# Projecting q, k and v in transposed layout, with rotary by VectorE shuffles across partitions

## The chip, the cores and the metric

The kernel runs on one core of a Trainium2 chip. The metric is the device time of one execution in microseconds (us). The engines of the core work side by side, each on its own list of instructions in order, and wait for each other by semaphores: TensorE (PE in the profile, its weight loads PEld), VectorE (DVE), ScalarE (ACT), GpSimd (POOL) and SyncE (SP, which issues most of the transfers).

## The reference

One decoder layer: 1024 tokens, model width 1024, all in float32. The part that matters here is the attention side of the token mixer, 8 query heads and 2 key/value heads of width 64, a window of 128 tokens:

```python
h = rmsnorm(x, pre_w_mix[l]) * (1.0 + sc1) + sh1
proj = h @ w_in[l]
aq, ak, av, hq, hf, hi, hg = jnp.split(proj, _SPLITS, axis=-1)
aq = partial_rope(aq.reshape(B, T, ATT_Q_HEADS, ATT_HEAD_DIM))
ak = partial_rope(ak.reshape(B, T, ATT_KV_HEADS, ATT_HEAD_DIM))
...
attn = sliding_window_sink_attention(aq, ak, av, attn_sinks[l])
attn = rmsnorm(attn, attn_out_w[l])
```

partial_rope turns only the first 16 of a head's 64 dimensions: with x1 the first eight and x2 the second eight, it gives x1·cos − x2·sin and x2·cos + x1·sin; the other 48 pass. In the window attention each block of 128 queries sees its own and the previous block of keys, with a mask and a sink per head in the softmax. Behind it follow a gated recurrence (hq, hf, hi, hg), an output projection and a squared-ReLU MLP; the change does not touch them.

## The kernel before

Tokens are cut into two halves of 512 and eight blocks of 128 (tb 0 to 7); the model width into eight column blocks of 128 (kb). Each float32 product is made of three products of split numbers, high by high, high by low, low by high, so each weight and each h has a tile "hi" and a tile "lo" (h: hhi, hlo; weights wq…h, wq…l, wkv…h, wkv…l). ScalarE writes hhi, POOL a helper f, VectorE hlo.

Stage 1, up to 57 us: x is normalised, turned and split for the first half, one kb at a time, and q and k/v of token blocks 0 to 3 are accumulated in step with it by first_mm: the h slice of one block is the weight operand, wq (512 columns) or wkv (256) moves, so the result has tokens on partitions. Stage 2, the loop with proj3, brings the second half of h and projects q of blocks 4 and 5 meanwhile. The rest of the second half's q and k/v are fillers: kv_later and q_later put single matmuls into a list feed_q, and feed(us) takes matmuls from it worth so many microseconds. Behind them the list holds values(tb), products pv for the recurrence.

Stage 3, from 72 to 185 us, is the attention. attention(tb) is a generator of eight steps per block: turn q and k by TensorE (pqT, pkT) so that the head dimension lies on partitions, and copy them out; scores sc for two head pairs; the mask (copy_predicated), maximum mx, its negative nm and sd on VectorE, eight exponentials on ScalarE, the sums den and their reciprocal, and the scaling of comb, half by VectorE, half by POOL; turn the probabilities (pT) and split them into pc (own block) and pp (previous block) on VectorE; the output oT; its squares' sum sqr, its sum over partitions ssp and ssc; the inverse root r_att by POOL, dg, rb. The loop over t interleaves the steps of blocks t, t+1 and t+2, with feed between them. VectorE also splits weights whv in it and sums products of the modulation (macc, by mod_sums).

The order is written by hand. pin holds an engine's instructions in the order of the program for a while; otherwise Queue.issue places an instruction behind a named one (marks: "kT", "sd", "rb", "dg"), and the scheduler fills in. Rotary before (rope) works on tokens on partitions: four small instructions (16 of 64 columns each head) for q and four for k of a block, on VectorE for blocks 0 and 1, on POOL for the others, with tables cosT and sinT of 64 KB each.

All instructions go through one helper, so nearly all rows of the profile carry its line, L39; rows are told apart by their tiles.

## Time and profile before

| | |
|---|---|
| time, median of 3 runs | 1082.05 us (1081.71 to 1082.11) |
| the profiled execution | 1081.48 us, span 1079.6 us |
| mean granted TensorE clock | 0.997 |
| TensorE busy | 1066.4 us, 99% of the span |
| VectorE busy | 806.3 us, 75% |
| ScalarE busy | 589.1 us, 55% |
| POOL busy | 372.8 us, 35% |
| 57 to 72 us | PE 15.00 of 15.0, DVE 13.07 |
| 72 to 105 us | PE 32.36 of 33.0, DVE 23.39 |
| 105 to 185 us | PE 79.35 of 80.0, DVE 64.21 |
| 185 to 1079 us | PE 886.06 of 894.0, DVE 668.86 |

The profile is of one execution. A row of a timeline gives the start, the busy time and the instruction with its output and inputs; in brackets follows the idle time of the engine before it and what ended that. The chain of waits goes back from the last instruction to what released each step. Spans of POOL are rough.

### The profile page before, as it was taken

To read this page: it belongs to the slowest core of one execution; us is meant where nothing else is said; L and a number is where in the kernel's file an instruction comes from. 1 tells how busy PE (TensorE), PEld (TensorE's weight loads), DVE (VectorE), ACT (ScalarE), POOL (GpSimd) and SP (SyncE) were. 2 spreads that over 40 slices of the span, in tenths; PEclk is the share of its full clock that TensorE was granted. 3 is DMA by queue.
4 is the path that set the end of the run, shared out by engine and by line. 5 is a ranking of instruction groups with operands and counts; after the bars stand their busy time and mean duration, and the time that the engine had idled before them with its cause. 6 is when DMAs were issued, how large, how long until landed. Compare 5 with 4: busy or idle time off the path is not lost.

```text
span 1079.6 us, 16058 instructions
## 1 busy us (share of the span) xinstructions
PE 1066.4 (99%) x5449; PEld 873.6 (81%) x5449; DVE 806.3 (75%) x1329; ACT 589.1 (55%) x1215; POOL 372.8 (35%) x497
## 2 busy tenths in 40 slices
PE   8999999999999999999999999999999999999996
PEld 6887777888888888888888888888888888888885
DVE  4877787879756655468867767786678887899776
ACT  4556544456547654566655555555664544456434
POOL 1263211233325643423444444443333333300014
PEclk9999999999999999999999999999999999999998
DMA  9904012444112342424676777767898888998537
GB/s 358 347 21 142 16 30 88 141 145 148 48 60 82 99 161 85 139 79 134 223 263 220 267 232 247 255 224 247 310 373 291 280 295 269 305 313 272 171 98 140
DMA packets 102979, 205.74 MB, mean 191 GB/s; under 512 B 13168, under 2 KB 13936, under 8 KB 102896
## 3 DMA queue, kind: packets, MB, share of 16 engines
q1 hardware_dynamic: 87408, 157.14, 43.1%
q0 software_dynamic: 15200, 47.20, 14.5%
q8 instruction: 43, 0.70, 0.3%
q10 hardware_dynamic: 288, 0.36, 0.1%
q14 instruction: 40, 0.33, 0.1%
HBM read 149.60 MB, written 55.05 MB: 190 GB/s over the span
## 4 chain that ended last, share of the span: by engine, by line
PE 93%; DMA 3%; DVE 2%; ACT 1%; issue 0%; SPq 0%; DVEq 0%; POOL 0%; ACTq 0%; POOLq 0%
PE pda L39 16%; PE pua L39 14%; PE pdc L39 8%; PE po L39 8%; PE puc L39 7%; PE phf L39 4%; PE phg L39 4%; PE pu L39 4%; PE phq L39 4%; PE pdb L39 4%; PE pv L39 4%; PE pub L39 4%; PE pq L39 2%; DMA wa<-wada 2%; PE pk L39 1%; PE sc L39 1%
## 5 line engine op out<-in xcount | busy, mean ns | idle before, releaser
L39 POOL TENSOR_TENSOR b<-b,b 128x512 f32<-128x512 f32 x64 | 88.5, 1383 | 217.2 <-DMA b<-w_dn 216.8
L39 ACT ACTIVATE dw<-dwr 128x512 fp32r<-128x512 f32 x72 | 45.4, 630 | 48.1 <-DMA dwr<-w_dn 25.0
L39 ACT ACTIVATE s<-s 128x512 f32<-128x512 f32 x84 | 52.9, 631 | 31.3 <-DVE s L39 30.0
L39 DVE TENSOR_TENSOR dw<-dwr,dw 128x512 fp32r<-128x512 f32 x72 | 53.7, 746 | 10.6 <-ACT dw L39 10.6
L39 DVE TENSOR_TENSOR acc<-pda,acc 128x512 f32<-128x512 f32 x68 | 47.0, 691 | 16.4 <-PE pda L39 15.9
L39 POOL TENSOR_TENSOR rrf<-ssf,mhalf 128x1 f32<-128x1 f32 x7 | 7.8, 1107 | 102.9 <-DVE ssf L39 102.9
L39 POOL DMA_DIRECT2D td<-b x64 | 36.3, 567 | 19.0 <-POOL b L39 19.0
L39 ACT ACTIVATE s<-pua 128x512 f32<-128x512 f32 x28 | 16.7, 597 | 40.8 <-PE pua L39 40.8
L39 DVE TENSOR_TENSOR wt<-s,wt 128x512 fp32r<-128x512 f32 x42 | 36.7, 873 | 2.6 <-ACT wt L39 2.4
L39 ACT ACT_TABLE_LOAD x28 | 35.9, 1283 | 1.7 <-PEq L1914 1.2
L39 DVE SCALAR_TENSOR_TENSOR macc<-wada,cs,macc 128x512 f32<-128x512 f32 x42 | 33.9, 807 | 1.9 <-DMA wada<-wada 1.0
L39 POOL DMA_DIRECT2D b<-w_dn x64 | 34.4, 540 | 2.5 <-issue 2.5
L39 ACT ACTIVATE comb<-comb,nm 128x128 f32<-128x128 f32 x64 | 24.8, 388 | 18.8 <-DVE sd L39 12.9
L39 DVE TENSOR_TENSOR wt<-a,wt 128x512 fp32r<-128x512 f32 x42 | 32.3, 769 | 0.9 <-ACT wt L39 0.9
L39 PE MATMUL pua<-bt_1h,wt 128*128 128x512 f32 x84 | 32.7, 389 | 0.0
L39 PE MATMUL pua<-bt_3h,wt 128*128 128x512 f32 x84 | 32.7, 389 | 0.0
L39 PE MATMUL pua<-bt_0h,wt 128*128 128x512 f32 x84 | 32.7, 389 | 0.0
L39 PE MATMUL pua<-bt_2h,wt 128*128 128x512 f32 x84 | 32.7, 389 | 0.0
L39 DVE TENSOR_TENSOR s<-puc,s 128x512 f32<-128x512 f32 x14 | 9.7, 691 | 27.9 <-issue 25.4
L39 ACT ACTIVATE wt<-s 128x512 fp32r<-128x512 f32 x42 | 26.3, 627 | 7.5 <-DVE s L39 7.3
L39 PE MATMUL pdc<-dw,du_3h 128*128 128x512 f32 x96 | 29.6, 389 | 0.0
L39 PE MATMUL pda<-dw,du_6h 128*128 128x512 f32 x96 | 29.6, 389 | 0.0
(768 smaller groups left out, 3749.1 us busy)
## 6 DMA issues: line engine op xcount, KB each, us to landing
dur<-ud SPq DMA_DIRECT2D x112, 256.0 KB, 4.4
wada<-wada SPq DMA_DIRECT2D x64, 256.0 KB, 3.3
b<-w_dn POOLq DMA_DIRECT2D x64, 256.0 KB, 5.0
td<-b POOLq DMA_DIRECT2D x64, 256.0 KB, 3.3
dwr<-td SPq DMA_DIRECT2D x64, 256.0 KB, 4.3
a<-w_u SPq DMA_DIRECT2D x56, 256.0 KB, 4.3
dwr<-w_dn SPq DMA_DIRECT2D x48, 256.0 KB, 4.5
ud<-s SPq DMA_DIRECT2D x42, 256.0 KB, 3.5
```

The source lines that it names most:

```text
L39: ins = op(*args, **kw)
```

## The change

The roles in the projections are exchanged: 128 columns of the weights are the weight operand, 512 tokens of h move, and the result has the head dimension on partitions at once. For each half there are six units u of 128 columns: four of q, one of k, one of v. ScalarE copies q and k to qT and kT (512 tokens each), and the turns pqT and pkT with their copies go. v comes out transposed as well (vT) and is turned by four TensorE transposes per half (v_turn), copied by ScalarE.

Rotary now works with dimensions on partitions, on whole 128x512 tiles: VectorE shuffles partitions within each 32 (dimensions 0 to 7 against 8 to 15) into sh, POOL multiplies sh by a sine table, which is zero where nothing is turned, VectorE multiplies the tile by a cosine table, which is one there, and then adds sh. There are ten such tiles: k and four q for each half. Five come before the attention, interleaved; five are placed behind marks "sd" and "pp" in it (rope_late). The tables are four tiles of 256 KB. The second half's k and v are projected in the loop of proj3, its four q units are the fillers. The attention's output gets tiles aT of its own. The feeds, the placing of the whv splits, and of the lower bound's small instructions (lmx, le ahead of the ropes, the others later) are set anew; marks "kT" become "sqr".

```diff
-    def first_mm(kb, tb, part, which=(0, 1)):
-        sl = slice(tb * P, tb * P + P)
-        ah, al = (h[:, sl] for h in hh[kb][0])
-        for w in which:
-            pst, (bh, bl), first, last = ((pk0[tb], wkv[kb], tb % 2 == 0, tb % 2 == 1) if w else
-                                          (pq0[tb], wq[kb], True, True))
+    def unit(u, kb):
+        w, c = (wq, u * P) if u < 4 else (wkv, (u - 4) * P)
+        return [h[:, c:c + P] for h in w[kb]]
+
+    def first_mm(kb, us, part, ts=slice(0, 512)):
+        bh, bl = (h[:, ts] for h in hh[kb][0])
+        for u in us:
+            pst, (ah, al) = pu[u][:, ts], unit(u, kb)
             if part == 0:
-                PE.matmul(pst, lhsT=ah, rhs=bh, start=(kb == 0 and first), stop=False)
-                PE.matmul(pst, lhsT=ah, rhs=bl, start=False, stop=False)
+                PE.matmul(pst, lhsT=ah, rhs=bh, start=(kb == 0 and ts.start == 0), stop=False)
+                PE.matmul(pst, lhsT=al, rhs=bh, start=False, stop=False)
             else:
-                PE.matmul(pst, lhsT=al, rhs=bh, start=False, stop=(kb == KB - 1 and last))
+                PE.matmul(pst, lhsT=ah, rhs=bl, start=False, stop=(kb == KB - 1))
...
         if kb == 6:
+            lbt = cload("lbt", [P, 2, 4], pool=tiny1)
+            cosT, sinT = ([load_raw(hv_, f"rope{i}_{th}", I["rope"][i, th]) for th in range(2)] for i in range(2))
...
-    def qproj(tb):
-        pq = pq0[tb]
-        q = m_(f"q{tb}")
-        ACT.activation(q, pq, AF.Copy, scale=0.125)
-        qn.append(q)
-
-    def kvproj(tb):
-        pk = pk0[tb]
-        kv = XA.tile([P, 256], F32, tag="kv", bufs=8, name=f"kv{tb}")
-        ACT.activation(kv, pk[:, :256], AF.Copy)
-        kvn.append(kv)
-
-    def rope(tb, nh, eng=POOL):
-        base = qn[tb] if nh == 8 else kvn[tb][:, 0:P]
-        v3 = base.rearrange("p (h d) -> p h d", d=64)
-        rt = t_(f"rt{tb}_{nh}", (P, 2, 8, 16))
-        t1, t2 = rt[:, 0], rt[:, 1]
-        cb = cosT[:, tb:tb + 1, :].broadcast_to([P, nh, 16])
-        s0 = sinT[:, tb:tb + 1, 0:8].broadcast_to([P, nh, 8])
-        s1 = sinT[:, tb:tb + 1, 8:16].broadcast_to([P, nh, 8])
-        eng.tensor_tensor(t1[:, :nh, :], v3[:, :, 0:16], cb, ALU.mult)
-        eng.tensor_tensor(t2[:, :nh, 0:8], v3[:, :, 8:16], s0, ALU.mult)
-        eng.tensor_tensor(t2[:, :nh, 8:16], v3[:, :, 0:8], s1, ALU.mult)
-        eng.tensor_tensor(v3[:, :, 0:16], t1[:, :nh, :], t2[:, :nh, :], ALU.add)
-
+    qs, ks, vs = [[], []], {}, {}
+
+    def evac(th, u, pst):
+        if u < 4:
+            t = m_(f"qT{th}_{u}")
+            qs[th].append(t)
+        else:
+            t = XA.tile([P, 512], F32, tag="kT", bufs=2, name=f"kT{th}") if u == 4 else t_(f"vT{th}")
+            (ks if u == 4 else vs)[th] = t
+        ACT.activation(t, pst, AF.Copy, scale=0.125 if u < 4 else 1.0)
+        return t
+
+    swap = [(i + 8) % 16 if i < 16 else i for i in range(32)]
+
+    def rope(x, th):
+        sh = t_("rope")
+        DVE.stream_shuffle(sh, x, swap)
+        POOL.tensor_tensor(sh, sh, sinT[th], ALU.mult)
+        DVE.tensor_tensor(x, x, cosT[th], ALU.mult)
+        yield
+        DVE.tensor_tensor(x, x, sh, ALU.add)
+        yield
+
+    def v_turn(th):
+        vT = vs[th]
+        pst = tp_ps(f"pvT{th}")
+        for j in range(4):
+            PE.transpose(pst[:, j * P:(j + 1) * P], vT[:, j * P:(j + 1) * P], ident)
+        vs[th] = XA.tile([P, 512], F32, tag="v", bufs=2, name=f"v{th}")
+        ACT.activation(vs[th], pst, AF.Copy)
...
-        q, kv = qn[tb], kvn[tb]
-        pqT = tp_ps(f"pqT{tb}")
-        for m in range(4):
-            PE.transpose(pqT[:, m * P:(m + 1) * P], q[:, m * P:(m + 1) * P], ident)
-        qT = t_(f"qT{tb}", [P, 4, P])
-        ACT.activation(qT, pqT.rearrange("p (m t) -> p m t", m=4), AF.Copy)
-        pkT = tp_ps(f"pkT{tb}")
-        PE.transpose(pkT[:, :P], kv[:, 0:P], ident)
-        kT = XA.tile([P, P], F32, tag="kT", bufs=3, name=f"kT{tb}")
-        marks["kT"] = DVE.tensor_copy(kT, pkT[:, :P]).ins
-        kTs[tb] = kT
-        yield
-        aw = q
-        a3 = aw.rearrange("p (m t) -> p m t", m=4)
...
-                        PE.matmul(scs[g][:, m, js], lhsT=qT[gs, 2 * mp + m, :], rhs=kTs[src][gs, :],
+                        PE.matmul(scs[g][:, m, js], lhsT=at(qs[tb // 4][2 * mp + m], tb, gs), rhs=at(ks[src // 4], src, gs),
...
-                PE.matmul(og, lhsT=kvn[tb - 1][:, vsl],
+                PE.matmul(og, lhsT=at(vs[(tb - 1) // 4], tb - 1)[:, gs],
                           rhs=pp[:, :, 2 * g:2 * g + 2, :].rearrange("p a m q -> p a (m q)"), start=True, stop=False)
-            PE.matmul(og, lhsT=kv[:, vsl], rhs=pc[:, :, 2 * g:2 * g + 2, :].rearrange("p a m q -> p a (m q)"),
+            PE.matmul(og, lhsT=at(vs[tb // 4], tb)[:, gs], rhs=pc[:, :, 2 * g:2 * g + 2, :].rearrange("p a m q -> p a (m q)"),
...
-    pq0.append(a_ps("pq4"))
+    pu1 = [a_ps("pk1")]
     for kb in range(KB):
         if 0 < kb < KB - 1:
             if kb + 2 < KB:
                 DVE.tensor_tensor(xT1[kb + 2], xT1[kb + 2], rbx, ALU.mult)
             first_evac(1, kb + 1, xT1[kb + 1])
-        (qproj if kb < 4 else kvproj)(kb % 4)
+        if kb < 6:
+            u = (0, 1, 5, 4, 2, 3)[kb]
+            evac(0, u, pu[u])
         if kb == 0:
-            pq0.append(mm_ps("pq5"))
-        for tb in (4, 5):
-            proj3(pq0[tb], htok(tb)[kb:kb + 1], wq[kb:kb + 1], kb == 0, kb == KB - 1)
-    for tb in range(4):
-        eng = DVE if tb < 2 else POOL
-        rope(tb, 8, eng)
-        rope(tb, 2, eng)
+            pu1.append(mm_ps("pv1"))
+        if kb == 5:
+            v_turn(0)
+        for u in (4, 5):
+            proj3(pu1[u - 4], [unit(u, kb)], [hh[kb][1]], kb == 0, kb == KB - 1)
+    for u in (5, 4):
+        evac(1, u, pu1[u - 4])
+    lmx = tiny1.tile([P, 4], F32, tag="lmx", bufs=1, name="lmx")
+    DVE.tensor_tensor(lmx, lbt[:, 0, :], lbt[:, 1, :], ALU.max)
+    le = small.tile([P, 2, 4], F32, tag="le", bufs=1, name="le")
+    DVE.tensor_tensor(le, lbt, lmx.unsqueeze(1).broadcast_to([P, 2, 4]), ALU.subtract)
+    ACT.activation(le, le, AF.Exp)
+    ropes = [rope(x, 0) for x in [ks[0]] + qs[0]]
+    for a, b in zip([None] + ropes, ropes + [None]):
+        if b:
+            next(b)
+        if a:
+            next(a)
...
+    late = [ks[1]]
+
+    def rope_late(mark):
+        old, DVE.last = DVE.last, marks[mark]
+        for _ in rope(late.pop(0), 1):
+            pass
+        DVE.last = old
+
+    def q_later(u):
+        pst = bank(f"pq1_{u}")
 
         def done():
-            pk0.append(pk())
-            kvproj(tb)
-            rope(tb, 2)
-
-        queue3(lambda: pk()[:, :256], htok(tb), wkv, 0.12, done)
-
-    def q_later(tb):
-        pq = bank(f"pq{tb}")
-
-        def done():
-            pq0.append(pq())
-            qproj(tb)
-            rope(tb, 8)
-
-        queue3(pq, htok(tb), wq, 0.227, done)
+            late.append(evac(1, u, pst()))
+
+        queue3(pst, [unit(u, kb) for kb in range(KB)], hhalf(1), 0.227, done)
...
-    feed(4.4)
+    feed(2.0)
+    v_turn(1)
+    feed(3.0)
     step(0)
-    feed(0.9)
+    feed(3.0)
     step(0)
-    step(0)
-    feed(4.8)
-    step(1)
-    feed(1.9)
+    rope_late("sd")
+    rope_late("sd")
+    feed(4.0)
     step(1)
     step(1)
-    feed(1.2)
...
         if t == 1:
-            old, DVE.last = DVE.last, marks["kT"]
-            split_hv(range(7, KB))
+            old, DVE.last = DVE.last, marks["sqr"]
+            split_hv(range(6, KB))
             DVE.last = old
         if 1 < t < 6:
-            mod_sums(2, "kT")
+            mod_sums(2, "sqr")
...
+        if t < 2:
+            rope_late("pp")
...
-    A["cosT"] = f(np.concatenate([co, co], 1).reshape(TB, P, 16).transpose(1, 0, 2))
-    A["sinT"] = f(np.concatenate([-si, si], 1).reshape(TB, P, 16).transpose(1, 0, 2))
+    rope = np.zeros((2, 2, 64, 1024), np.float32)
+    rope[0, :, 16:] = 1.0
+    rope[0, :, :16] = np.concatenate([co, co], 1).T
+    rope[1, :, :16] = np.concatenate([-si, si], 1).T
+    A["rope"] = f(rope.reshape(2, P, 2, 512).transpose(0, 2, 1, 3))
```

The order on TensorE just ahead of the first scores (sc), before: pk are the fillers, pqT and pkT the turns of block 0.

```order
L39 MATMUL pqT_1041<-c_tab,q_832 128x128 x4
L39 MATMUL pkT_1048<-c_tab,kv_893 128x128
L39 MATMUL pk_1027<-wkv2l,hhi_1_872 128x256
L39 MATMUL pk_1027<-wkv2h,hlo_1_873 128x256
L39 MATMUL pk_1027<-wkv2h,hhi_1_887 128x256
L39 MATMUL pk_1027<-wkv2l,hhi_1_887 128x256
L39 MATMUL pk_1027<-wkv2h,hlo_1_888 128x256
L39 MATMUL pk_1027<-wkv3h,hhi_1_902 128x256
L39 MATMUL pk_1027<-wkv3l,hhi_1_902 128x256
L39 MATMUL pk_1027<-wkv3h,hlo_1_903 128x256
L39 MATMUL sc_0_0_1062<-kT_1050,qT_1046 128x128
```

And now (pq_0 is the second half's first q unit, a filler):

```order
L39 MATMUL pq_0_955<-hhi_1_879,wq6l 128x512
L39 MATMUL pq_0_955<-hhi_1_900,wq7h 128x512
L39 MATMUL pq_0_955<-hlo_1_901,wq7h 128x512
L39 MATMUL sc_0_0_988<-kT_855,qT_0_809 128x128
L39 MATMUL sc_0_1_989<-kT_855,qT_0_809 128x128
L39 MATMUL sc_0_0_988<-kT_855,qT_1_825 128x128
L39 MATMUL sc_0_1_989<-kT_855,qT_1_825 128x128
L39 MATMUL pq_0_955<-hhi_1_900,wq7l 128x512
```

The turns are gone, and the scores come behind 23 of the 24 products of that unit, without the copies of pqT and pkT between.

On VectorE behind the last hlo of the second half, before (q_832, kv_893: block 0; q_848: block 1):

```order
L39 SCALAR_TENSOR_TENSOR hlo_1_917<-xT_7_756,a_130,f_7_919 128x512
L39 TENSOR_TENSOR rt_8_938<-q_832,c_cosT 128x128
L39 TENSOR_TENSOR rt_8_938<-q_832,c_sinT 128x8x8 x2
L39 TENSOR_TENSOR q_832<-rt_8_938 128x8x16
L39 TENSOR_TENSOR rt_2_943<-kv_893,c_cosT 128x32
L39 TENSOR_TENSOR rt_2_943<-kv_893,c_sinT 128x2x8 x2
L39 TENSOR_TENSOR kv_893<-rt_2_943 128x2x16
L39 TENSOR_TENSOR rt_8_948<-q_848,c_cosT 128x128
L39 TENSOR_TENSOR rt_8_948<-q_848,c_sinT 128x8x8 x2
L39 TENSOR_TENSOR q_848<-rt_8_948 128x8x16
L39 TENSOR_TENSOR rt_2_953<-kv_908,c_cosT 128x32
```

And now (rope is the shuffled tile sh, rope_0_739 and rope_1_741 are cosine tables):

```order
L39 SCALAR_TENSOR_TENSOR hlo_1_901<-xT_7_735,a_130,f_7_903 128x512
L39 TENSOR_TENSOR lmx<-c_lbt 128x4
L39 TENSOR_TENSOR le<-c_lbt,lmx 128x8
L39 STREAM_SHUFFLE rope<-kT_855 128x512
L39 TENSOR_TENSOR kT_855<-kT_855,rope_0_739 128x512
L39 STREAM_SHUFFLE rope<-qT_0_809 128x512
L39 TENSOR_TENSOR qT_0_809<-qT_0_809,rope_0_739 128x512
L39 TENSOR_TENSOR kT_855<-kT_855,rope 128x512
L39 STREAM_SHUFFLE rope<-qT_1_825 128x512
L39 TENSOR_TENSOR qT_1_825<-qT_1_825,rope_0_739 128x512
L39 TENSOR_TENSOR qT_0_809<-qT_0_809,rope 128x512
L39 STREAM_SHUFFLE rope<-qT_2_870 128x512
```

The small rotary of two blocks is replaced by shuffles and multiplications of whole tiles; between a tile's cosine multiplication and its addition stand another tile's shuffle and cosine.

On VectorE behind the first block's maximum, before (comb is the probabilities, whose scaling by rd releases pT):

```order
L39 COPY_PREDICATED comb_1060<-c_mle,sc_1_1_1071 128x256
L39 TENSOR_REDUCE mx_1078<-comb_1060 128x8
L39 TENSOR_TENSOR mx_1080<-mx_1078,c_sinks 128x8
L39 TENSOR_SCALAR nm_1082<-mx_1080 128x8
L39 TENSOR_TENSOR sd_1084<-c_sinks,mx_1080 128x8
L39 COPY kT_1143<-pkT_1141 128x128
L39 TENSOR_TENSOR den_1097<-sm_1088,es_1086 128x8
L39 RECIPROCAL rd_1099<-den_1097 128x8
L39 TENSOR_TENSOR comb_1060<-comb_1060,rd_1099 128x512
L39 COPY_PREDICATED comb_1166<-c_mle,sc_0_0_1167 128x256
```

And now (kT_920 and qT_0_997: the second half's k and first q unit):

```order
L39 TENSOR_TENSOR sd_1027<-c_sinks,mx_1023 128x8
L39 STREAM_SHUFFLE rope<-kT_920 128x512
L39 STREAM_SHUFFLE rope<-qT_0_997 128x512
L39 TENSOR_TENSOR kT_920<-kT_920,rope_1_741 128x512
L39 TENSOR_TENSOR qT_0_997<-qT_0_997,rope_1_741 128x512
L39 TENSOR_TENSOR kT_920<-kT_920,rope 128x512
L39 TENSOR_TENSOR qT_0_997<-qT_0_997,rope 128x512
L39 TENSOR_TENSOR den_1040<-sm_1031,es_1029 128x8
L39 RECIPROCAL rd_1042<-den_1040 128x8
L39 TENSOR_TENSOR comb_986<-comb_986,rd_1042 128x512
```

Two late ropes stand between sd and den, where the copy of kT stood.

More of the change, by code (lines that the diff above doesn't have):

```diff
@@ L380, in hybrid_layer, with idle @@
     spare_ps = tp_ps("spare")
-    def idle(n):
+    def idle(n, dst=None):
         for _ in range(n):
-            PE.matmul(spare_ps, lhsT=ones_r, rhs=spare, start=True, stop=True)
+            PE.matmul(spare_ps if dst is None else dst, lhsT=ones_r, rhs=spare, start=True, stop=True)
     idle(11)
@@ L454, in hybrid_layer @@
     norm_scale(0, 0, ACT, (3,))
-    idle(4)
+    idle(4, a_ps("spare2"))
     mod_mm((0, 1), range(2))
@@ L460, in hybrid_layer @@
     first_part(1)
-    pq0 += [tp_ps("pq2"), tp_ps("pq3")]
-    pks.append(tp_ps("pk23"))
-    pk0 += [pks[1][:, i * 256:i * 256 + 256] for i in range(2)]
     first_wq(1)
-    for tb in (2, 3):
-        first_mm(0, tb, 0, (0,))
+    first_mm(0, range(4), 0, ts1)
     mod_fold((0, 1))
@@ L469, in hybrid_layer @@
     xT0.append(first_T(0, 1))
-    for tb in (2, 3):
-        first_mm(0, tb, 0, (1,))
-    for tb in (2, 3):
-        first_mm(0, tb, 1)
+    first_mm(0, (4, 5), 0, ts1)
+    first_mm(0, range(6), 1, ts1)
     nextq = {1: (1, 0)}
@@ L498, in hybrid_layer @@
             pin(False, SP)
-        for tb in range(3):
-            first_mm(kb, tb, 0)
+        first_mm(kb, range(4), 0)
         if q:
@@ L688, in attention @@
             if tb:
-                DVE.tensor_tensor(pp[:, mp], pT3, pc[:, mp], ALU.subtract)
+                marks["pp"] = DVE.tensor_tensor(pp[:, mp], pT3, pc[:, mp], ALU.subtract).ins
         spread(tb - 1)
@@ L704, in attention @@
         sqr = small.tile([P, P], F32, tag="sqr", bufs=1, name=f"sqr{tb}")
-        DVE.tensor_reduce(sqr, sq.rearrange("p (m t) -> p t m", m=4), AX.X, ALU.add)
+        marks["sqr"] = DVE.tensor_reduce(sqr, sq.rearrange("p (m t) -> p t m", m=4), AX.X, ALU.add).ins
         yield
@@ L770, in values, with values_all @@
         queue3(pv, htok(tb), whv, 0.227, done)
+    def values_all():
+        values(0)
+        a = len(feed_q) - 6
+        rest = feed_q[a:]
+        del feed_q[a:]
+        values(1)
+        feed_q[-6:-6] = rest
+        for tb in range(2, TB):
+            values(tb)
     a2 = tiny1.tile([P, KB], F32, tag="a2", name="a2")
@@ L779, in hybrid_layer @@
         mods += [modcols(3, half, m_, sh2), modcols(4, half, m_, sc2)]
-    for tb in (4, 5):
-        qproj(tb)
-        rope(tb, 8)
-    for tb in (4, 5):
-        kv_later(tb)
-    for tb in (6, 7):
-        q_later(tb)
-        kv_later(tb)
+    for u in range(4):
+        q_later(u)
     def step(tb):
@@ L857, in hybrid_layer @@
     hgw = cload("hgw", [P, 1], pool=tiny1)
-    lbt = cload("lbt", [P, 2, 4], pool=tiny1)
-    lmx = tiny1.tile([P, 4], F32, tag="lmx", bufs=1, name="lmx")
-    DVE.tensor_tensor(lmx, lbt[:, 0, :], lbt[:, 1, :], ALU.max)
-    le = small.tile([P, 2, 4], F32, tag="le", bufs=1, name="le")
-    DVE.tensor_tensor(le, lbt, lmx.unsqueeze(1).broadcast_to([P, 2, 4]), ALU.subtract)
-    ACT.activation(le, le, AF.Exp)
+    DVE.last = marks["sqr"]
     lsum = tiny1.tile([P, 4], F32, tag="lsum", bufs=1, name="lsum")
@@ L871, in hybrid_layer @@
     DVE.tensor_tensor(lcs, lp[:, 0, :], lp[:, 1, :], ALU.add)
+    DVE.last = None
     lb = tiny1.tile([P, 4], F32, tag="lb", name="lb")
```

40 lines of the change are left out of this document (17 added, 23 removed).

## Prediction

> **What bounds the kernel now.** The page first: busy time by engine, then the chain that ended last.
>
> ```profile
> span 1079.6 us, 16058 instructions
> PE 1066.4 (99%) x5449; PEld 873.6 (81%) x5449; DVE 806.3 (75%) x1329; ACT 589.1 (55%) x1215; POOL 372.8 (35%) x497
> PE 93%; DMA 3%; DVE 2%; ACT 1%; issue 0%; SPq 0%; DVEq 0%; POOL 0%; ACTq 0%; POOLq 0%
> ```
>
> TensorE is 99% busy and carries the end. By this alone each microsecond taken from TensorE would come off. But shares are averages, and the change sits at 57 to 185 us. So next the chain of waits cut to that stretch (start, length, engine and tile):
>
> ```profile
> 59.98 8.16 PE pq L39 x36
> 68.14 4.43 PE pk L39 x37
> 72.57 0.44 PE pqT L39 x4
> 73.01 0.11 PE pkT L39
> 73.12 0.95 PE pk L39 x8
> 74.07 1.09 PE sc L39 x16
> ...
> 105.29 1.95 PE oT L39 x8
> 107.23 0.59 PE pqT L39 x4
> 107.82 0.11 PE pkT L39
> ...
> 143.20 1.94 PE oT L39 x8
> ...
> 155.81 1.95 PE oT L39 x8
> ```
>
> One token block of attention takes 155.81 − 143.20 = 12.61 us, with TensorE never out of work. VectorE's timeline of the same period (start, busy, instruction, then idle before it and its releaser):
>
> ```profile
> 141.77 1.28 DVE L39 TENSOR_TENSOR pp<-pT,pc 128x512 f32<-128x512 f32 x2
> ...
> 145.21 0.17 DVE L39 TENSOR_TENSOR den<-sm,es 128x8 f32<-128x8 f32 x1 [1.56 <-ACT comb L39]
> ...
> 147.87 0.28 DVE L39 COPY kT<-pkT 128x128 f32<-128x128 f32 x1
> 148.06 1.53 DVE L39 SCALAR_TENSOR_TENSOR macc<-wada,cs,macc 128x512 f32<-128x512 f32 x2
> 149.51 0.29 DVE L39 TENSOR_REDUCE ssc<-ssp 128x1 f32<-128x128 f32 x1
> ...
> 150.75 0.28 DVE L39 TENSOR_SCALAR dg<-c_tab,r_att 128x128 f32<-128x128 f32 x1 [0.25 <-POOL r_att L39]
> ...
> 154.38 1.28 DVE L39 TENSOR_TENSOR pp<-pT,pc 128x512 f32<-128x512 f32 x2
> ```
>
> It idles twice, for ScalarE's exponentials (which follow VectorE's own maximum) and for POOL's power, never for TensorE. Its loop from pp to pp is 154.38 − 141.77 = 12.61 us by its own work and those two latencies. Here both engines are the bound at once: TensorE made shorter would only wait for pp.
>
> **TensorE's share of the change.** A 512-column product costs 8.16/36 = 0.227 us, a 256-column one 4.43/37 = 0.120. The second half had 4 × 24 of each: 96 × (0.227 + 0.120) = 33.3 us. It now has 6 × 24 × 0.227 = 32.7: −0.6. The first half changes the same way, but much of it stands ahead of a transfer:
>
> ```profile
> 34.57 5.04 DMA x<-x
> ...
> 41.02 0.77 ACT hhi L39
> ```
>
> The products of 41.84 follow that hhi, so TensorE saved before it is absorbed: zero. The turns of q and k go: twice 0.44 + 0.11 and six times 0.59 + 0.11 = 5.3 us. Two turns of v come, 0.44 each: +0.9. The sum is −5.0 us.
>
> The rotary tables, 1 MB on SP's queue, come behind the x loads and ahead of the eight xT loads; 0.6 MB that stood there (old tables, two whv loads) goes or moves behind xT. The windows (busy time and count of PE, PEld, DVE, ACT, POOL, then clock, DMA share, GB/s):
>
> ```profile
> 48.00:52.00 4.00, 4.00 (x27) 3.55 (x26) 2.06 (x4) 1.47 (x4) 1.37 (x2) 1.00 1.01 332
> ...
> 56.00:60.00 4.00, 4.00 (x21) 3.33 (x20) 3.16 (x6) 3.46 (x6) 2.04 (x3) 1.00 0.00 0
> ```
>
> So xT lands 0.4 MB later at 332 GB/s, 1.2 us, and queues that fell empty before 56 have room for whv. TensorE's work on the first half runs until 57 and hides it: nothing; without that cover, 1.2 us.
>
> At 0.2 us a kT copy, VectorE's loop falls to 12.4 us, TensorE's to 12.61 − 0.70 = 11.9.
>
> **VectorE's share** is the open one. Rows of before at this place:
>
> ```profile
> 65.88 0.75 DVE L39 SCALAR_TENSOR_TENSOR hlo<-xT,a,f 128x512 fp32r<-128x512 f32 x1 [0.78 <-POOL f L39]
> 66.55 0.29 DVE L39 TENSOR_TENSOR rt<-q,c_cosT 128x128 f32<-128x128 f32 x1
> ...
> 72.62 0.25 DVE L39 TENSOR_SCALAR omlb<-lb 128x4 f32<-128x4 f32 x1
> ...
> 75.16 1.45 DVE L39 COPY_PREDICATED comb<-c_mle,sc 128x256 f32<-128x256 int32 x4 [1.72 <-PE sc L39]
> 76.64 1.22 DVE L39 TENSOR_REDUCE mx<-comb 128x8 f32<-128x1024 f32 x1
> ...
> 78.19 0.24 DVE L39 TENSOR_TENSOR sd<-c_sinks,mx 128x8 f32<-128x8 f32 x1
> 80.86 0.29 DVE L39 COPY kT<-pkT 128x128 f32<-128x128 f32 x1 [2.43 <-PE pkT L39]
> 81.69 0.17 DVE L39 TENSOR_TENSOR den<-sm,es 128x8 f32<-128x8 f32 x1 [0.54 <-ACT comb L39]
> ...
> 122.72 0.48 DVE L39 TENSOR_SCALAR macc<-wada,cs 128x512 f32<-128x512 f32 x1
> ```
>
> The small rotary ran 66.55 to 70.4, and none of it delayed TensorE. It is replaced by ten ropes of three VectorE instructions and one of POOL on 128x512, five of them ahead of the first score. A 512-column two-input instruction starts 0.60 us after the one before (pp: two in 1.28). No row of before has a shuffle; the nearest is mx, 1.22 for 1024 one-input columns, so about 0.6 for 512; the ends are 0.48, the one-input macc row, and 1.2, the whole mx. I take 0.6, by mx.
>
> POOL's multiply is the other unknown, and the trace shows what happens when it meets VectorE:
>
> ```profile
> 92.44 0.69 DVE L39 TENSOR_TENSOR comb<-comb,rd 128x512 f32<-128x512 f32 x1
> 93.05 1.53 DVE L39 TENSOR_TENSOR whv1l<-whv1r,whv1h 128x512 fp32r<-128x512 f32 x1
> ```
>
> ```profile
> 92.55 1.48 POOL L39 TENSOR_TENSOR comb<-comb,rd 128x512 f32<-128x512 f32 x1 [2.93 <-ACT whv1h L39]
> ```
>
> whv1l took 1.53 where comb, of the same form, took 0.69. POOL was issued at 92.55 under comb, which ended its reading near 93.05; POOL then ran to 94.03, 0.98 us, and whv1l's 0.6 began there and ended at 94.58. That is one at a time: a two-input VectorE instruction and POOL's excluded each other. The Trainium skill, "SBUF — State Buffer", section "Who interferes with whom", states this as a rule: a VectorE instruction with two SBUF inputs and a GpSimd instruction that reads SBUF want one read port, and whichever issues second blocks fully, while a one-input VectorE instruction keeps clear. The rows agree for the two-input side; without the rule and the row the sum below would be that of the second rival.
>
> In the new order, each tile's shuffle releases POOL just as VectorE issues its cosine multiply, which goes first. POOL (0.98) follows, and the next two-input instruction, another tile's cosine or the add, waits for it. So a rope costs shuffle 0.6 + cosine 0.6 + POOL 0.95 + add 0.6 = 2.75 us rather than 1.8, whichever tiles are interleaved.
>
> Start: on ScalarE the v copy stands ahead of hhi of the last column block, 0.6 us by this row:
>
> ```profile
> 67.49 1.28 ACT L39 ACTIVATE q<-pq 128x512 f32<-128x512 f32 x2 [1.89 <-PE pq L39]
> ```
>
> so hlo is 0.6 later, two lower-bound instructions follow (0.5), and the ropes start at 66.55 + 1.1 = 67.65.
>
> 1. First score. TensorE reaches it at 57.2 + 71 × 0.227 (48 for k and v, 23 of the first q unit) + 0.44 + about 0.35 for the late hlo = 74.1. It needs k, q0 and q1; q1's add is the eleventh of VectorE's fifteen rope instructions, behind four shuffles and four cosines, 3.6 ropes: 67.65 + 3.6 × 2.75 = 77.6. Stall 3.5.
> 2. Softmax of block 0. All five ropes end at 67.65 + 5 × 2.75 − 0.35 = 81.1, and the masks start there rather than at 75.16, 5.9 late. 3.0 later (sd) two late ropes are queued, six instructions, 3.6 + one POOL wait 0.95; den starts at 88.7 rather than 81.69, 7.0 late. Behind it on VectorE are comb's scaling, the masks of block 1, pc, and so TensorE's pT, oT and rb. TensorE has seven more fillers ahead, and VectorE's idle in this stretch gives a little back. Walking the same rows one by one: stalls 1.0 at pT0, 2.0 at oT0, 1.1 at rb0, 0.4 at oT1, together 4.5.
> 3. The loop. TensorE would need 11.9, VectorE gives 12.4: 0.5 in each of three periods, 1.5.
>
> Stalls 9.5, less 5.0 of work: +4.5. The profiled execution took 1081.48 us, 1.9 more than its span, and the median is 1082.05; 1081.48 + 4.5 = 1086.0, and 1086.6 from the median. I leave it at 1086.0. After 185 us TensorE has no gap that could win this back.
>
> **Rivals.**
>
> *TensorE's work alone decides.* Everything on VectorE and POOL is covered, no new stall: −5.0, 1076.5. For it: 99% and 93%. Against it: the loop above, where VectorE waits for no TensorE instruction, and five 512-column ropes where 3.9 us of small rows stood. It decides only if the ropes end before 74.1, which needs under 1.3 us each, and if VectorE's loop is shorter than it looks.
>
> *VectorE's chain without contention.* Ropes at 1.8: q1 is added at 67.65 + 3.6 × 1.8 = 74.1, a stall of 0.1; all end at 76.7, the masks are 1.6 late, den 83.6 instead of 81.69. Then about 2.6 of stalls up to oT1 and 1.5 in the loop: 4.2 − 5.0 = −0.8, 1080.7. This is the side that is not slower: the gain is eaten, little more. It decides if POOL and VectorE overlap freely. Against it is whv1l; for it, that POOL's rows in the stage are rough.
>
> *The shuffle costs double.* At 1.2 us, three shuffles more ahead of the first score and five ahead of the masks add 3.0, the late ones, partly under the exponentials, about 1: 1086.0 + 4 = 1090. The Trainium skill, "VectorE: DVE Perf Modes", section "The perf-mode tier table", gives about 2400 ns for 2048 columns; an estimate by that would be 0.6 to 0.7 for 512, and no row of before shows it.
>
> **How the numbers follow.** Contention with a 0.6 us shuffle 0.50 (own range 1083.5 to 1089: half or one and a half times the excess of contention); no contention 0.20; TensorE alone 0.18; slow shuffle 0.12. A measurement of this kernel tells 0.2%, 2.2 us, from no change: under 1079.9 is faster, over 1084.2 slower. Faster: nearly all of 0.18, and a quarter of the 0.20: 0.22. Same: most of the rest of it, and an eighth of the first case: 0.20. Slower: 0.58. The range runs from 1077, leaving half of TensorE alone below, to 1090.5, leaving half of the slow shuffle above.
>
> **What would show it.** The five ropes on VectorE: start near 67.7, shuffles of 0.6, cosines or adds of 1.5 where a POOL multiply runs beside them; the first sc near 77.6 with a wait on VectorE's add of 3.5; oT near 112 for block 1 instead of 105.29; in the loop, waits of TensorE on pp or sqr of 0.5 a period. Cosines and adds that stay at 0.69 beside running POOL multiplies would make the contention wrong, and the time near 1081. A loop that falls to 11.9 us would make VectorE's bound wrong. Shuffles over 1 us would be the third rival.

## The result

The changed kernel takes 1092.81 us (median of five runs, 1091.16 to 1093.29) where the kernel before takes 1081.82 (1081.71 to 1082.11). The ratio is 1.0099, with a 95% interval of 1.0084 to 1.0113: slower, and by 11.0 us rather than the 4.5 forecast. The time lies 2.3 us above the range. The profiled execution took 1092.65 us, 11.2 more than that of before. Of the executions below, two at 1330 us and one of the kernel before at 2172 us were in a slower state and are left out of ranges and ratios.

The page of the changed kernel, by engine, and the engines' shares of the chain that ended last:

```profile
PE 1068.2 (98%) x5339; PEld 867.1 (79%) x5339; DVE 818.8 (75%) x1345; ACT 585.4 (54%) x1205; POOL 373.9 (34%) x459
PE 83%; DVE 7%; ACT 2%; POOL 1%; issue 1%; DVEq 0%; ACTq 0%; POOLq 0%
```

TensorE has 110 instructions fewer and is still busy 1.8 us longer; VectorE's share of the chain went from 2% to 7%. So two things are to be found: where TensorE waits, and why fewer instructions take longer. The first product of the output projection tells where to look. Before, then after:

```profile
349.90 0.48 PE L39 MATMUL po<-wo_0h,mx 128*128 128x512 f32 x1
```

```profile
361.15 0.48 PE L39 MATMUL po<-wo_0h,mx 128*128 128x512 f32 x1
```

It starts 11.25 us later, all that the span has grown (from 1079.6 to 1090.8). The time is lost ahead of it, and none is lost or won back behind it. TensorE's waits over the whole program, by what ended them (total, times, longest), in the kernel after:

```profile
PE sc L39 <- DVE qT L39: 3.6, 2, 2.6
PE oT L39 <- DVE pp L39: 2.1, 6, 0.5
PE oT L39 <- ACT comb L39: 2.0, 1, 2.0
...
PE rb L39 <- DVE dg L39: 0.7, 1, 0.7
PE pT L39 <- DVE comb L39: 0.7, 1, 0.7
```

Of these, the kernel before has one:

```profile
PE oT L39 <- DVE pp L39: 0.4, 1, 0.4
```

VectorE's timeline of the changed kernel shows what TensorE waits for (start, busy, instruction, idle before and its releaser):

```profile
68.20 0.73 DVE L39 STREAM_SHUFFLE rope<-kT 128x512 f32<-128x512 f32 x1
68.96 0.69 DVE L39 TENSOR_TENSOR kT<-kT,rope 128x512 f32<-128x512 f32 x1
...
73.76 2.38 DVE L39 TENSOR_TENSOR qT<-qT,rope 128x512 f32<-128x512 f32 x2
76.07 0.72 DVE L39 STREAM_SHUFFLE rope<-qT 128x512 f32<-128x512 f32 x1
...
79.12 0.01 DVE L39 LOAD_MASK_SELECT rope<-qT  x1
...
82.77 0.76 DVE L39 COPY_PREDICATED comb<-c_mle,sc 128x256 f32<-128x256 int32 x2
86.25 0.78 DVE L39 COPY_PREDICATED comb<-c_mle,sc 128x256 f32<-128x256 int32 x2 [2.72 <-PE sc L39]
...
88.60 0.16 DVE L39 TENSOR_TENSOR sd<-c_sinks,mx 128x8 f32<-128x8 f32 x1
...
94.19 0.15 DVE L39 TENSOR_TENSOR den<-sm,es 128x8 f32<-128x8 f32 x1
```

and POOL's timeline shows one of its multiplies there:

```profile
73.80 1.79 POOL L39 TENSOR_TENSOR rope<-rope,rope 128x512 f32<-128x512 f32 x1 [1.29 <-DVE rope L39]
```

A lone two-input instruction takes 0.69 (68.96), and two in a row took 1.28 before. The two at 73.76 take 2.38, with POOL's sine multiply inside them. One rope follows the other by 79.12 − 76.07 = 3.05 us: 0.76 for the shuffle, twice 0.6, and so 1.1 for POOL. POOL's own row says 1.79; 0.6 of that is the time in which the cosine was reading, so that the row seems to count POOL's wait as well. The five ropes take 82.77 − 68.20 = 14.6 us.

TensorE at the same time, and the windows of the stretch (busy time and count of PE, PEld, DVE, ACT, POOL, then granted clock, DMA share, GB/s):

```profile
76.19 0.49 PE L39 MATMUL sc<-kT,qT 64*128 64x128 f32 x4 [1.00 <-DVE qT L39]
79.24 0.80 PE L39 MATMUL sc<-kT,qT 64*128 64x128 f32 x4 [2.56 <-DVE qT L39]
...
82.27 0.63 PE L39 MATMUL pq<-hlo,wq1h 128*128 128x512 f32 x1
82.69 0.63 PE L39 MATMUL pq<-hhi,wq1l 128*128 128x512 f32 x1
...
84.71 0.40 PE L39 MATMUL pq<-hlo,wq3h 128*128 128x512 f32 x1
84.95 0.40 PE L39 MATMUL pq<-hhi,wq3l 128*128 128x512 f32 x1
...
85.51 0.71 PE L39 MATMUL sc<-kT,qT 64*128 64x128 f32 x8
...
101.70 1.98 PE L39 MATMUL oT<-pc,v 128*64 128x512 f32 x4 [2.03 <-ACT comb L39]
```

```profile
74.00:80.00 6.00, 2.44 (x15) 1.48 (x13) 5.93 (x9) 0.00 (x0) 3.38 (x3) 0.81 0.00 0
80.00:85.00 5.00, 5.00 (x15) 3.94 (x14) 3.53 (x5) 0.60 (x1) 3.91 (x4) 0.54 0.15 32
...
101.00:106.00 5.00, 4.30 (x12) 2.27 (x13) 4.93 (x9) 3.39 (x9) 1.48 (x1) 0.66 0.07 17
```

From 80 to 85 us TensorE is busy all the time, at a granted clock of 0.54. Products follow each other by 82.69 − 82.27 = 0.42 us, not by the 0.24 of 84.71 to 84.95. The clock fell after waits of 1.00 and 2.56 us. The window 101 to 106 shows 0.66, after a wait of 2.03 us at the first oT, where four oT took 1.98 us instead of 1.08. (The row of that wait names ScalarE's comb. But VectorE's pc, which oT reads, ends at 101.56, and in the six of these kernels that have this wait oT starts 0.14 to 0.15 behind the end of pc: it is VectorE again, held up there by a late rope.) The Trainium skill, "TensorE: Matmul & The Clock Gate", section "Part 1: The HAM clock gate (the "warmup" mystery)", says that an idle TensorE falls to half rate and must be busy for a window of about 3.4 us before it is released. The trace agrees on the release: its records of the granted clock give half rate from 77.73 to 84.56 and from 101.62 to 105.04, 6.83 and 3.41 us. It differs on the fall, for which the table of the Trainium skill there has an idle window of about 3.4 us: waits of 2.56 and 2.03 us were enough here. The prediction had no such term.

Last, the loop. Its pp rows, one block apart, are those quoted of before:

```profile
141.91 1.28 DVE L39 TENSOR_TENSOR pp<-pT,pc 128x512 f32<-128x512 f32 x2
...
154.20 1.28 DVE L39 TENSOR_TENSOR pp<-pT,pc 128x512 f32<-128x512 f32 x2
```

The period is 12.29 us, against 12.61.

**Where the 11.2 us are.** Each TensorE instruction of 57 to 202 us was charged with the time from its start to the next one's start, less the wait in it, and these were added up by tile. Waiting grew from 1.0 to 9.9 us: +8.9. The turns of q and k, 4.05, went, and those of v, 0.71, came; products take 0.2 more in the kernel without rotary below, where the clock is 1.00: together −3.1. Products, scores, pT and oT take 4.8 longer, nearly all of it while the clock was at half: TensorE worked from 79.24 to 84.56 and from 101.70 to 105.04 of that time, and half of these 8.7 us is 4.3. The stretch begins 0.55 later; in the profiles of three of the kernels below it begins only 0.2 to 0.3 later, so that part of this belongs to the one execution. 8.9 − 3.1 + 4.8 + 0.55 = 11.15. This says where the time lies, not what caused it: with less time in slow products TensorE could wait longer instead.

### The profile page after: what moved, and what is told of

Its sections match the earlier page's. It is cut to its first block, busy times and chain, and to the rows that moved or that the text cites. A ratio compares the mean times of both kernels' runs of the same rounds, so it can differ in the third digit from the quotient of the medians.

```text
span 1090.8 us, 15818 instructions
## 1 busy us (share of the span) xinstructions
PE 1068.2 (98%) x5339; PEld 867.1 (79%) x5339; DVE 818.8 (75%) x1345; ACT 585.4 (54%) x1205; POOL 373.9 (34%) x459
## 4 chain that ended last, share of the span: by engine, by line
PE 83%; DVE 7%; ACT 2%; POOL 1%; issue 1%; DVEq 0%; ACTq 0%; POOLq 0%
PE pda L39 16%; PE pua L39 14%; PE pdc L39 8%; PE po L39 8%; PE puc L39 7%; PE phg L39 4%; PE pu L39 4%; PE phq L39 4%; PE pdb L39 4%; PE phf L39 4%; PE pub L39 3%; PE o L39 1%; ACT comb L39 1%; PE pq L39 1%; DVE mx L39 1%; DVE comb L39 1%
## 5 line engine op out<-in xcount | busy, mean ns | idle before, releaser
L39 DVE TENSOR_TENSOR acc<-pdc,acc 128x512 f32<-128x512 f32 x36 | 24.6, 684 | 7.4 <-PE pdc L39 7.3
L39 PE MATMUL pda<-dw,du_7h 128*128 128x512 f32 x96 | 29.6, 389 | 0.0
```

Source lines behind the costliest of these rows:

```text
L39: ins = op(*args, **kw)
```

## The experiments

The kernel before was run beside each; its median was 1081.65 to 1081.80 us in every group, so that a median is read against 1081.7.

### What makes the start late

**Both score pairs together.** The fillers between the two score pairs of block 0 move ahead of the first.

```diff
-    feed(3.0)
-    step(0)
-    feed(3.0)
-    step(0)
+    feed(6.0)
+    step(0)
+    step(0)
     rope_late("sd")
```

> The changed kernel with the 13 filler products that stood between the two score pairs of block 0 moved ahead of the first pair; all else as changed. Theory A (late ropes, then a second score pair queued behind fillers, then a half clock on TensorE after its long wait): the first mask pair stays near 82.8 us, the second comes right behind it instead of at 86.25, so sd comes near 85.5 instead of 88.6, and the time falls by 2 to 4 us from 1092.8. Rival B (only the amount of VectorE and TensorE work counts, where single products stand doesn't matter): within 1 us of 1092.8.

1089.98 us (1089.73 to 1090.15), ratio 1.0075 (1.0058 to 1.0091): 2.8 less than the changed kernel, as the first theory said. sd comes at 85.73 rather than 88.60.

**TensorE kept at work through the wait.** Seventeen products without use stand ahead of the first score.

```diff
     feed(3.0)
+    idle(17, a_ps("warm"))
     step(0)
```

> The changed kernel with 17 idle products of 512 columns (about 3.9 us at full clock, results unused) ahead of the first score of block 0, in the stall. Theory A: they cost nothing, since TensorE waits there anyway; the granted clock in 80 to 85 us goes from 0.54 to 1.0, the 13 fillers behind take 3.0 instead of 5.5 us, and the time falls by 2 to 3 us though work was added. Rival B (the clock plays no part, or the stall is not there): the time stays within 1 us, or rises by up to 3.9 us.

1090.17 us (1089.39 to 1090.70), ratio 1.0076 (1.0061 to 1.0091): work was added and 2.6 us went. Of this kernel, the window, the second score pair on TensorE, and VectorE up to sd:

```profile
80.00:85.00 5.00, 5.00 (x27) 3.83 (x26) 4.69 (x8) 0.35 (x1) 3.48 (x4) 1.00 0.24 57
```

```profile
82.63 0.71 PE L39 MATMUL sc<-kT,qT 64*128 64x128 f32 x8
```

```profile
83.38 0.78 DVE L39 COPY_PREDICATED comb<-c_mle,sc 128x256 f32<-128x256 int32 x2 [0.28 <-PE sc L39]
...
85.73 0.16 DVE L39 TENSOR_TENSOR sd<-c_sinks,mx 128x8 f32<-128x8 f32 x1
```

The ropes are as slow as before, but the clock stays at 1.00, the second pair comes at 82.63 instead of 85.51, and sd at the same 85.73 as in the kernel above. The kernel with both pairs together keeps the half clock, from 81.64 to 88.48, and this one keeps the fillers between the pairs; both are rid of the same time. So neither the fillers nor the half clock costs sd much alone: at full clock the second mask waits 0.28. Together they cost about 2.5; the other 0.4 of the 2.9 by which sd is earlier is that the ropes began earlier in these two executions (67.86 and 67.70 against 68.20).

**The sine multiply on VectorE.**

```diff
-        POOL.tensor_tensor(sh, sh, sinT[th], ALU.mult)
+        DVE.tensor_tensor(sh, sh, sinT[th], ALU.mult)
```

> The changed kernel with the sine multiplication of all ten ropes on VectorE instead of POOL. Theory A (POOL's multiply and VectorE's two-input instructions exclude each other, about 1.1 us per rope of waiting): a rope becomes 0.75 + 3 x 0.60 = 2.55 us instead of 3.05, the five end near 81 instead of 82.8 us, no VectorE multiply of a rope is recorded over 0.8 us, and the time falls by 2 to 5 us (part of it by a shorter first stall and less half clock). Rival C (the two engines overlap freely and the long rows are waits for something else): VectorE gets 0.6 us more per rope and the time rises by 3 to 6 us.

The runs lay between 1088.91 and 1091.20 us, ratio 1.0078 (1.0061 to 1.0095): some 2 less than the changed kernel, at the small end of what was expected. These runs spread over 2.3 us and those of the changed kernel over 2.1, so that the size of the gain is not sure. In VectorE's timeline no rope instruction is blocked any more:

```profile
74.97 0.01 DVE L39 LOAD_MASK_SELECT rope<-qT  x1
...
76.33 1.28 DVE L39 TENSOR_TENSOR qT<-qT,rope 128x512 f32<-128x512 f32 x2
77.54 0.01 DVE L39 LOAD_MASK_SELECT rope<-qT  x1
```

A rope now takes 77.54 − 74.97 = 2.57 us, with all four instructions on VectorE, against 3.05 with one of them given to POOL. Handing the multiply to POOL cost VectorE more time in a rope than doing it.

### What the parts of the change cost

**No rotary at all.** Projections, layout and the turns of v stay as changed.

```diff
         sh = t_("rope")
-        DVE.stream_shuffle(sh, x, swap)
-        POOL.tensor_tensor(sh, sh, sinT[th], ALU.mult)
-        DVE.tensor_tensor(x, x, cosT[th], ALU.mult)
         yield
-        DVE.tensor_tensor(x, x, sh, ALU.add)
         yield
```

> The changed kernel with all rotary instructions left out (the shuffles, the sine and cosine multiplications and the additions of all ten tiles), so attention works on unrotated q and k; layout, tables' loads and order of the rest stay. Theory A: the excess is the ropes' alone; TensorE waits under 1 us at the first scores, no half clock, and what is left is TensorE's 5.0 us saved as far as VectorE's loop of 12.4 us lets it through: 1076.5 to 1080 us. Rival D (the transposed layout itself costs time: longer products, the turns of v, the tables' loads): 1082 us or more.

1082.18 us (1081.48 to 1082.94, ten runs), ratio 1.0000 (0.9991 to 1.0009). This is a miss: 1076.5 to 1080 was expected. Even with no rotary on VectorE, TensorE's shorter work brings nothing. The loop's period is that of the full kernel, 12.3 us, and TensorE's waits in the attention are:

```profile
PE rb L39 <- DVE dg L39: 2.0, 2, 1.3
...
PE oT L39 <- DVE pp L39: 1.1, 4, 0.4
```

It is the number that the rival had forecast, by which the layout itself costs time. But the layout's work is shorter: of the 3.1 us saved, waits took back 2.3 (3.3 against 1.0 in the whole stretch), and slower scores and a later beginning 0.2 each, so that the output projection starts at 349.62 against 349.90. The longest of these waits, 1.3 at rb of block 0, may depend on where the fillers stand; so 1082 is the floor of this order, and is not shown to be that of the layout.

**Only the first five ropes left out.**

```diff
+        if not th:
+            yield
+            yield
+            return
         sh = t_("rope")
```

> The changed kernel without the rotary of the first half's five tiles; the five late ropes stay, so attention of blocks 0 to 3 works on unrotated q and k. Theory A (what comes late at the start is carried to the end, and the late ropes stretch VectorE's chain as well): sd of block 0 at 81.8 us as without any rope, den some 2 us later than there because of the two ropes behind sd, and a total between no rope at all (1082.2) and the change (1092.8), 1085 to 1088. Rival E (the late ropes lie in VectorE's waits for the exponentials and cost nothing): 1081.5 to 1083.5.

1086.15 us (1085.80 to 1087.89), ratio 1.0042 (1.0029 to 1.0055), as expected. The late five cost 1086.15 − 1082.18 = 4.0 us although they stand beside exponentials; the first five, then, 6.7.

**The sine multiply left out.** All thirty rope instructions of VectorE stay.

```diff
-        POOL.tensor_tensor(sh, sh, sinT[th], ALU.mult)
```

> The changed kernel with the sine multiplication left out of all ten ropes (shuffle, cosine, addition stay, POOL does nothing for them), so that VectorE keeps its 30 rope instructions and meets no POOL multiplication in them. It is the prediction's second rival made real (ropes without contention), which gave 1080.7. Theory A (that rival left out the fillers between the score pairs; contention is about half of the ropes' price): a rope 0.76 + 0.60 + 0.60 = 1.97 us, the five end near 77.8, k, q0 and q1 near 75.2 where TensorE arrives, no half clock at the start, oT of block 0 near 96, and 1085 to 1088. Rival C (contention is all of it): 1080 to 1083. Rival B (contention is nothing, the amount of VectorE work all): above 1090.

1083.19 us (1082.61 to 1085.54, ten runs), ratio 1.0014 (1.0005 to 1.0024). The first theory's 1085 to 1088 is missed, and the rival that puts everything on contention was 0.2 short of it. On VectorE a rope now takes 75.20 − 73.21 = 1.99 us:

```profile
73.21 0.74 DVE L39 STREAM_SHUFFLE rope<-qT 128x512 f32<-128x512 f32 x1
...
75.20 0.01 DVE L39 LOAD_MASK_SELECT rope<-qT  x1
```

VectorE's thirty instructions cost 1.0 us more than none. POOL's ten, with all that follows from them (clock included), cost 1092.81 − 1083.19 = 9.6. Not all of that is the price of sharing: with the ten on VectorE the kernel above took 1090.7.

**POOL writes, and reads nothing.** That run takes away two things, POOL's reading and the add's wait for POOL's result. Here the multiply becomes two memsets of the same tile, so that the wait stays.

```diff
-        POOL.tensor_tensor(sh, sh, sinT[th], ALU.mult)
+        POOL.memset(sh, 0.0)
+        POOL.memset(sh, 0.0)
```

> The changed kernel with POOL's sine multiplication of each rope replaced by two fills of the same tile (zeros, about 0.94 us together, by the 0.94 us of the 1024-column fill of comb), so that POOL still works behind each shuffle and each addition still waits for it, but POOL reads nothing; the rotary's partner is lost. Theory P (what stretches the ropes is that VectorE's two-input instructions and POOL's reads exclude each other): the ropes are as short as without the sine (2.0 us, the five end near 77.8), no cosine or addition over 0.8 us among the first five, and the time is 1083 to 1085. Rival W (VectorE's additions simply wait for POOL's result, whatever POOL does): ropes of about 3 us as in the change, and 1089 or more.

1083.47 us (1083.24 to 1084.16, ten runs), ratio 1.0017 (1.0007 to 1.0026), as the theory said. The timelines of POOL and of VectorE in this kernel:

```profile
72.61 1.11 POOL L39 MEMSET rope<- 128x512 f32 x2 [0.88 <-DVE rope L39]
```

```profile
72.58 1.29 DVE L39 TENSOR_TENSOR qT<-qT,rope 128x512 f32<-128x512 f32 x2
73.80 0.01 DVE L39 LOAD_MASK_SELECT rope<-qT  x1
```

POOL works for 1.11 us beside the two instructions at 72.58, about as long as its share of a rope was, and they take 1.29 rather than 2.38. It is POOL's reading that stops VectorE. The Trainium skill, "SBUF — State Buffer", section "Who interferes with whom", says so too: a VectorE instruction with two SBUF inputs collides with a GpSimd instruction that reads SBUF, "not with one that only writes it".

### Why the shorter TensorE work brings nothing

Two kernels take the sums of the modulation (macc) off VectorE in the loop and leave them to be done behind it: the first without any rotary, the second the kernel before.

```diff
-        if 1 < t < 6:
-            mod_sums(2, "sqr")
```

> The changed kernel without any rotary (as before in the run without ropes, 1082.2 us), and with VectorE's modulation sums of blocks 2 to 5 taken out of the attention loop to behind it. Theory F (in the transposed layout the loop is bound by VectorE, 12.3 us a block against TensorE's 11.9): the blocks 2 to 5 fall to 11.5 to 12.0 us each and the time to 1080 to 1081. Rival G (the loop is bound by TensorE or by a latency that the sums don't touch): the period stays 12.3 and the time within 0.5 us of 1082.2.

> The kernel before the change with the same sums taken out of its loop. Theory F: TensorE itself needs 12.6 us a block there, so the period stays at 12.6 and the time within 0.7 us of before. Rival H (VectorE alone bounds the loop of before too): the period falls by up to 1 us a block and the time by 2 to 4 us.

Without rotary: 1090.37 us (1089.64 to 1092.15), ratio 1.0079 (1.0066 to 1.0092). Kernel before: 1089.74 us (1089.08 to 1091.25), ratio 1.0073 (1.0060 to 1.0086). Both times miss what was expected, and a wait that neither expectation had decides them. The sums, left to the end, delay the recurrence: TensorE waits 7.5 us for VectorE's sg without rotary, and 5.4 in the kernel before so edited. The periods are what these runs can still tell. Two oT of successive blocks, without rotary, then of the kernel before so edited:

```profile
144.22 1.08 PE L39 MATMUL oT<-pp,v 128*64 128x512 f32 x4
...
156.36 1.09 PE L39 MATMUL oT<-pp,v 128*64 128x512 f32 x4
```

```profile
143.03 1.08 PE L39 MATMUL oT<-pp,kv 128*64 128x512 f32 x4
...
155.64 1.09 PE L39 MATMUL oT<-pp,kv 128*64 128x512 f32 x4
```

The blocks ahead of them started at 132.06 and 130.43, and TensorE waits for VectorE in neither loop. So TensorE itself needs 12.15 us a block in the new layout (11.5 to 12.0 was expected) and 12.60 in the old. The turns and copies of a block were worth 0.45, not the 0.70 of the prediction. VectorE with its sums allows 12.3, which takes another 0.15 of that 0.45; the rest went into the waits named above.

### Can the start be repaired?

**Ropes in another order, late ropes spread out.** Three shuffles first, then cosines, then adds. The late ropes stand one by one, the second of them behind the next block's sd. Fillers move from behind the second score pair to between the pairs, the first half's v turn moves behind one more column block, and the macc sums leave the loop.

```diff
         DVE.stream_shuffle(sh, x, swap)
         POOL.tensor_tensor(sh, sh, sinT[th], ALU.mult)
+        yield
         DVE.tensor_tensor(x, x, cosT[th], ALU.mult)
...
-    for a, b in zip([None] + ropes, ropes + [None]):
-        if b:
-            next(b)
-        if a:
-            next(a)
+    for j in (0, 1, 2, 0, 1, 2, 0, 1, 2, 3, 4, 3, 4, 3, 4):
+        next(ropes[j])
...
-    feed(3.0)
+    feed(4.5)
     step(0)
     rope_late("sd")
-    rope_late("sd")
-    feed(4.0)
+    feed(2.5)
```

> The changed kernel, complete, with another order: k, q0 and q1 shuffled first, then their cosines, then their additions, then q2 and q3 the same way (so that POOL's multiplications run beside one-input shuffles); 20 instead of 13 fillers between the score pairs; the first v turn one column block later (ScalarE's v copy behind the last hhi); one late rope behind each of five places rather than two behind the first; and the modulation sums of blocks 2 to 5 behind the loop. Theory A: k, q0 and q1 are done 7.7 us after the ropes' start instead of 11, near 75; first stall under 1 us, no half clock at the start, oT of block 0 near 96 instead of 101.7, and the time 1083 to 1087. Rival B (the amount of VectorE work alone decides): 1089 or more.

1099.43 us (1098.61 to 1100.10), ratio 1.0159 (1.0146 to 1.0173): the worst of all, though the start was mended. The first scores come at 74.88 without a wait, and the first oT at 93.39 instead of 101.70. What was won is lost behind it, as TensorE's waits show:

```profile
PE phq L39 <- DVE sg L39: 7.6, 1, 7.6
PE pv L39 <- DVE whv5l L39: 3.9, 1, 3.9
```

Its rows in the timelines of POOL and of VectorE show which VectorE instructions POOL stops:

```profile
68.36 4.70 POOL L39 TENSOR_TENSOR rope<-rope,rope 128x512 f32<-128x512 f32 x3 [1.85 <-issue]
```

```profile
68.77 0.76 DVE L39 STREAM_SHUFFLE rope<-qT 128x512 f32<-128x512 f32 x1
69.42 0.80 DVE L39 TENSOR_TENSOR kT<-kT,rope 128x512 f32<-128x512 f32 x1
70.14 3.48 DVE L39 TENSOR_TENSOR qT<-qT,rope 128x512 f32<-128x512 f32 x2
```

The shuffle, with one input, runs beside POOL undisturbed. The last two of the two-input cosines take 3.48 rather than 1.28.

**The same with the sums back in the loop, and whv's block 5 split earlier.**

```diff
-            split_hv(range(3, 5))
+            split_hv(range(3, 6))
...
-        if t == 0:
-            split_hv(range(5, 6))
```

> The reordered complete kernel (shuffles first, 20 fillers between the score pairs, first v turn later, late ropes one by one) with the modulation sums back in the loop and all of the weights whv split before the products that need them. Theory A: without the wait of TensorE for whv5l (3.9 us), the half clock behind it and the wait for the sums behind the loop (7.6 us), the time falls from 1099.4 to 1085 to 1088; not below before, since the run without any rope took 1082.2. Rival B: the waits only move, 1090 or more.

The runs lay between 1089.48 and 1092.09 us, ratio 1.0071 (1.0050 to 1.0093). TensorE's waits have moved, as the rival said:

```profile
PE ssp L39 <- DVE sqr L39: 4.1, 3, 2.1
PE oT L39 <- DVE pp L39: 3.1, 7, 1.0
```

**Only the first five ropes reordered.** The late ropes, the sums and whv stay as in the change; rope order, v turn and the fillers between the score pairs are those of the reordered kernel.

> The changed kernel, complete, with another order of the first five ropes alone (three shuffles, three cosines, three additions, then two of each), 20 instead of 13 fillers between the score pairs of block 0 (and 11 instead of 18 behind), and the first v turn one column block later; the late ropes stand where the change has them. Theory A (late start, fillers between the score pairs and half clock cost some 6 us): first scores near 75 without a wait, oT of block 0 near 96 instead of 101.7, and 1085 to 1088. Rival B (what is won at the start is lost behind, since the late ropes meet POOL in any case): 1090 or more.

1088.51 us (1088.26 to 1088.82), ratio 1.0062 (1.0045 to 1.0079): 4.3 less than the changed kernel, the most that a complete kernel of this layout reached, and half a microsecond above the expected 1085 to 1088. The first score no longer waits; the first pT waits 3.3 us for comb instead. None of these kernels comes near the kernel before.

## Why the prediction was right in kind and too small

**Right: what bounds the stretch.** VectorE's chain did carry the lateness to TensorE, and POOL's multiply and VectorE's two-input instructions did exclude each other. The row of before on which this rested (whv1l, 1.53) was enough, and the run with a POOL that only writes confirms the mechanism.

**Right, in part by luck: the stalls.** Forecast were 3.5 at the first score, 1.0 at pT0, 2.0 at oT0, 1.1 at rb0, 0.4 at oT1, and 1.5 in the loop. Measured were 3.6; 0.7 and 0.2 at pT; 2.0; none at rb0 and at oT1; 1.7 more than before on pp; and 0.7 at the last block's rb, which was not forecast. In all 9.5 were forecast, and waiting grew by 8.9. The first stall came out because both of its ends were late, TensorE by 1.1 and q1's add by 1.6 us.

**Wrong: the start of block 0's softmax, since a stall was costed at its length.** This is the step that failed. Item 2 let the masks run where the ropes ended, at 81.1, as if all scores of block 0 were done by then, and had no term for what the stall does to the clock. But thirteen fillers stood between the two score pairs. The clock fell within the stall, at 77.73, and at half clock the fillers took until 85.51. The second mask therefore came at 86.25, sd at 88.60 instead of 84.1, den at 94.19 instead of 88.7. The runs with both pairs together and with useless products each take one half of this away; both have sd at 85.73, and 2.6 to 2.8 us of the total go. That much is shown to hang on this step, of the 6.8 between 1086.0 and the measured median. The 4.8 us of slower work are not its price: the kernel with useless products is at full clock up to 1084 us, the one with both pairs together is not, and they take the same time within 0.2 us. At full clock TensorE waited instead, or ran the useless products.

**Wrong by 1.9 us: the term of TensorE's work, −5.0.** It measured −3.1. Each turn was priced at its rows in the chain of waits, 0.59 + 0.11 a block. TensorE pipelines, and a small matmul overlaps its neighbours: start to start, the turns of a block took 0.51, and the two periods without the macc sums differ by 0.45. The 0.6 us from wider products did not come at all. In the kernel without rotary −5.0 would have given 1076.5; it took 1082.18, since waits took back 2.3 of the 3.1 there.

**Small: the size of a rope.** 2.75 was forecast and 3.05 measured. The shuffle is 0.76 rather than 0.6 from start to start, and POOL's part 1.1 rather than 0.95. (With an instruction on another tile behind it, as in three of the late ropes, a shuffle does take 0.61 to 0.66; here the cosine of the same tile follows.) For five ropes that is 1.5 us. Nearly all of it stayed without effect on the first stall, since TensorE too arrived 1.1 later, at 75.2. It did delay the masks: even with both pairs together and with useless products the ropes end at 82.42 and 82.34 instead of 81.1.

**Of the same kind as forecast: the loop.** VectorE set its period at 12.29, against 12.4, and TensorE waits 0.2 to 0.5 a block for pp.

**The rivals.** *TensorE's work alone*, 1076.5: refuted, 1082.2 without any rotary. *No contention*, 1080.7: the kernels in which POOL reads nothing are this case, and they took 1083.2 and 1083.5; the 2.5 to 2.8 above are mostly the 1.9 by which TensorE's saving was overpriced in this sum too. *A shuffle of 1.2 us*: refuted, 0.73. Its time of 1090 was the nearest to the result, for another reason.

**Open.** About 1 us of the miss was not taken apart. The five runs of the changed kernel spread over 2.1 us, those of before over 0.4. The fastest of the five, 1091.16, has the highest mean clock, 0.997 against 0.993 to 0.995, which fits a fall of the clock that varies from run to run; no run tested it. The late ropes' 4.0 us owe nothing to the clock: in the kernel without the first five it stays at 1.00 to 1079.84 us. Most of them come with POOL's multiply, since without it all ten ropes together cost 1.0; a run with the late ropes alone and no multiply would split them for sure.
